# Fewer, larger DMAs around the RWKV systems of a hybrid decoder step

## The chip, the cores and the metric

The kernel runs on one core of one Trainium2 chip. The metric is the device time of one execution in microseconds. Each core has five engines that run their own instruction queues: PE (matrix products; its weight loads are shown as PEld), DVE (vector), ACT (scalar), POOL (GpSimd) and SP, which in this kernel issues every DMA.

## What is computed

One inference step of a two-layer trunk on 1104 tokens (64 sample tokens, 16 meta tokens, 1024 prompt tokens) of width 1024. Layer 0 is gated DeltaNet. Layer 1, which the change touches, is RWKV-7 time mixing over 16 heads of 64:

```python
rkvz = einsum('sbtd,sde->sbte', xs[:4], w_rkvz)      # r, k, v, z projections of mixed tokens
w = -softplus(-(w0 + tanh(xs[4] @ w1) @ w2)) - 0.5   # vector decay
a = sigmoid(a0 + (xs[5] @ a1) @ a2)
kk = l2norm((k * k_k).reshape(B, T, H, N))
k = k * (1.0 + (a - 1.0) * k_a)
decay = exp(-exp(w)); b = kk * a
def step(S, inp):                                     # per token, state S is [value, key]
    S = S*d_t + einsum('bhvk,bhk->bhv', S, -kk_t)[..., None]*b_t + v_t[..., None]*k_t
    return S, einsum('bhvk,bhk->bhv', S, r_t)
```

After it come a per-head GroupNorm, a bonus term, a SiLU gate, an output projection and a final RMSNorm.

## The kernel before

Tokens lie along the free dimension, features on the 128 partitions, in three segments of 384, 384 and 336 tokens. The recurrence is done in chunks of 64 tokens: within a chunk the rank-one updates form a unit lower triangular system, whose inverse is needed before the recurrence can run. A *system* here is one pair of heads (8 pairs, `p`) in one segment (3, `s`): 24 systems, numbered `n = 8 * s + p`, each with 6 chunks of 64 tokens for two heads.

Layer 1 has three stages.

1. `keys_decay_rate` projects the keys and computes the decay sums (cumulative, per chunk) and `a`, and writes them to DRAM: `kd`, `csd`, `ad`, each [8, 128, 1152]. Zeros are put in the last 48 columns of all but `csd`.
2. `layer1` runs 24 projections (`project`: r, then v, then z, 8 feature tiles each; `rd`, `vd`, `zd` in DRAM). After projections 1, 4, 7, 10 and 13 of them stands a call of `rwkv_inverse`, which does five systems (the last call four). For every system, or *item*, it loads `cs`, `a` and `k` (`rwkv_load`, an item ahead), scales the keys to `kk` (`skk` in the profile), takes exponentials of the decay sums on ACT (`sDp`, `siD`), squares the keys (`sgl`), forms alpha = kk * Dp (`sal`, DVE L1285, with column fixes on POOL) and bk = kk * a * iD in place (POOL L1310, DVE L1311), and stores both to DRAM (`ald`, `bkd`) for stage 3. PE makes the 12 products of 64x64 that give the triangular blocks (`fL`) and the squared norms of the keys per head (`frss`, a product with a mask of two columns, `hmask`). The blocks go to DRAM (`rltd`), the norms through a copy (`rkc`, DVE L1327) too (`rssd`). After five items, `block_scale` loads the norms and inverts them, `inverse_blocks` loads all 32x32 diagonal blocks of the batch in one tile (`invA`), `inverse32` inverts them on DVE with 62 small steps (`invtmp`, `invT`, L452 and L454), and the results go through DRAM (`r_t`, `r_u`) into `T1n` and into the tiles `sTT`, one per system, in four DMAs for each. `inverse_merge` then joins the blocks (`mY`, `invY`, `mU`), POOL scales them (L1336), and they are stored (`ttd`).
3. `wave` runs the recurrence, the output projection and the final norm. `rwkv_front` starts one system every two steps: it loads `cs`, `k`, `a`, `r`, `v` (`fld...`), `alpha` and `bk` (into `AR` and `BK`) and later the inverse (`rTT`).

All tiles come from pools. A tag with `bufs` buffers is reused round-robin: the next user of a buffer waits until its last reader is done, a DMA among them. The order of instructions on each engine is fixed at compile time: a scheduler simulates the program's timeline and takes what is ready by priority, roughly program order; in the wave, PE's order is written by hand. So moving a call in the program, or changing a size, gives a new order on every engine. The instructions that split weights in a high and a low part (`whi` on ACT L86, `wlo` on POOL L90) and mix tokens (`mixs`) run beside the inverse.

`inverse_blocks` and the tag `invA` at L465 serve the RWKV batches alone; layer 0 has a buffer of that name of its own (L641) and calls `inverse32` directly.

Of the kernel before, what the change touches and what calls it, by code (L numbers as in the profile page):

```python
# [35 lines left out]
class Builder:  # L36
# [76 lines left out]
    def consts(self):  # L113
        nc, i = self.nc, self.i
        cp = self.cp = self.ctx.enter_context(self.tc.tile_pool(name="consts", bufs=1))
        self.psum = ExitStack()
        self.psum_pool()
        t = self.t
        self.ident = t(cp, [128, 128], "ident")
        make_identity(nc, self.ident)  # L120
        vals = [1.0, -0.5]
        self.cvals = t(cp, [128, len(vals)], "cvals")
        self.cidx = {}
        for n, v in enumerate(vals):
# [5 lines left out]
        nc.gpsimd.memset(self.hmask, 0.0)  # L130
        for h in (0, 1):
            nc.gpsimd.memset(self.hmask[64 * h:64 * h + 64, h:h + 1], 1.0)
# [324 lines left out]
    def inverse_blocks(self, name, ltd, scale_blk, pool, TT, T1n, L21, nth):  # L457
# [7 lines left out]
        A = self.t(pool, [128, 1024], "invA", 2)[0:nb]  # L465
# [746 lines left out]
    def rwkv_masks(self, ap, first=False):  # L1212
# [14 lines left out]
        if first:  # L1227
            self.m_strs2 = t(ap, [128, 64], "m_strs2")
            mask(self.m_strs2, True)
            return  # L1230
# [17 lines left out]
    def rwkv_open(self):  # L1248
        self.rk2 = self.t(self.cp, [128, 144], "rk2")
        self.csd, self.ad, self.rd, self.vd, self.zd, self.kd = (self.dram([8, 128, 1152], n) for n in  # L1250
                                                                 ("csd", "ad", "rd", "vd", "zd", "kd"))
        self.ttd, self.ald, self.bkd = (self.dram([24, 128, 384], n) for n in ("ttd", "ald", "bkd"))

    def rwkv_load(self, n, pool, tag, names):
        nc, t = self.nc, self.t
        s, p = divmod(n, 8)
        c0 = SEGS[s][0]
        ld = {}
        for nm in names:
            d = {"cs": self.csd, "a": self.ad, "r": self.rd, "v": self.vd, "k": self.kd}[nm]  # L1260
            ld[nm] = t(pool, [128, 384], tag + "ld" + nm, 2 if nm in "rv" or tag == "s" else 1)
            nc.sync.dma_start(ld[nm], d[p][:, c0:c0 + 384])
        return ld

    def rwkv_keys(self, p, ld, pool, tag):

        nc, t = self.nc, self.t
        kk = t(pool, [128, 384], tag + "kk", 2)
        self.act(kk, ld["k"], AF.Identity, scale=self.pcol["rwkv_k_k"][:, p:p + 1])
        return kk, *self.rwkv_decays(ld, pool, tag)  # L1270

    def rwkv_decays(self, ld, pool, tag):
# [4 lines left out]
        self.act(Dp[:, 1:385], ld["cs"], AF.Exp, scale=-self.DEC)  # L1277
        self.act(iD, ld["cs"], AF.Exp, scale=self.DEC)
# [14 lines left out]
    def rwkv_inverse(self, b, pool):  # L1293
# [4 lines left out]
        ltd, ssd = self.dram([nth, 128, 64], f"rltd{b}"), self.dram([nth, 128], f"rssd{b}")  # L1298
        for q, n in enumerate(items):
            s, p = divmod(n, 8)  # L1300
            names = ("cs", "a", "k")
# [6 lines left out]
            al = t(pool, [128, 6, 64], "sal", 1)  # L1308
            self.alpha(al, kk, Dp, s, nc.vector)
            nc.gpsimd.tensor_tensor(kk, kk, ld["a"], op=ALU.mult)  # L1310
            nc.vector.tensor_tensor(kk, kk, iD, op=ALU.mult)  # L1311
            nc.sync.dma_start(self.ald[n], al.rearrange("p c k -> p (c k)"))
            nc.sync.dma_start(self.bkd[n], kk)
            gp = self.ps("f", 2, "L")
            ssp = self.ps("f", 2, "rss")
            for c in range(6):
                for h in (0, 1):
                    a = 64 * h
                    self.mm(gp[a:a + 64, 64 * c:64 * c + 64], kk[a:a + 64, 64 * c:64 * c + 64], al[a:a + 64, c, :])
            self.mm(ssp[0:2, 0:384], self.hmask, sq)  # L1320
# [5 lines left out]
            kc = t(pool, [2, 384], "rkc", 1)  # L1326
            nc.vector.tensor_copy(kc, ssp[0:2, 0:384])  # L1327
# [12 lines left out]
    def rwkv_front(self, p, s):  # L1340
# [11 lines left out]
        ld = self.rwkv_load(P.n, fp, "f", ("cs", "k", "a", "r", "v"))  # L1352
# [7 lines left out]
        nc.sync.dma_start(AR[:, 0].rearrange("p c k -> p (c k)"), self.ald[P.n])  # L1360
        nc.sync.dma_start(BK[:, :, 1, :], self.bkd[P.n].rearrange("p (c k) -> p c k", k=64))
# [439 lines left out]
    def layer1(self, ctx, right, stay, xa, xb, x):  # L1801
# [9 lines left out]
        for n, (m, k) in enumerate(todo):  # L1811
# [3 lines left out]
            if n in (1, 4, 7, 10, 13):  # L1815
                self.rwkv_inverse((1, 4, 7, 10, 13).index(n), ip)
# [160 lines left out]
```

## Time and profile before

| | |
|---|---|
| median of 3 runs | 2365.65 us (2362.40 to 2366.57) |
| the profiled execution | 2362.64 us, span 2360.9 us |
| busy: PE, PEld | 2167.1 us (92%), 1961.9 us (83%) |
| busy: DVE, ACT, POOL | 1571.2 us (67%), 1282.6 us (54%), 949.4 us (40%) |
| mean granted TensorE clock | 0.964 |
| DMA | 308.9 MB in 499,719 packets, 45.6% of 16 engines' span |

Times in the profile are microseconds from the span's start. A line of a group reads: source line, engine, operation, out<-in by the program's names, shape, count, then busy time and mean ns of one, then idle time of that engine just before and what ended it. A line of the chain of time begins with start and duration. A line of waits reads: engine and tile that waited, what it waited for, total us, times, the longest. A line "min/median/max" gives durations in ns. "issue" means that the profile shows nothing waited for. SPq lines are DMA issues; their duration is the time to issue, not to land.

### The profile page before, as it was taken

What the parts mean: (1) busy time and instruction counts of PE and PEld (TensorE: products, weight loads), DVE (VectorE), ACT (ScalarE), POOL (GpSimd) and SP (SyncE); (2) the same over time, 40 slices, a digit from 0 to 9 for tenths busy, and PEclk for the clock granted to TensorE, in tenths of its full rate; (3) what the DMA queues carried; (4) which work ended last, traced back from release to release, by engine and by line L of the source; (5) the groups of instructions that cost most, each with busy time, mean ns of one, the idle gap of its engine ahead of it and who ended that gap; (6) DMA issues with size and microseconds to landing.
All of it is one profiled execution on the core that took longest, in us unless ns stands there. A gap on an engine that the chain in (4) does not pass through costs nothing. (4 is left out here: it accounts for less than half of the span.)

```text
span 2360.9 us, 54503 instructions
## 1 busy us (share of the span) xinstructions
PE 2167.1 (92%) x19737; PEld 1961.9 (83%) x19737; DVE 1571.2 (67%) x4219; ACT 1282.6 (54%) x3599; POOL 949.4 (40%) x1318
## 2 busy tenths in 40 slices
PE   6989999999999999999999999999888888899886
PEld 5888989889898989898989998887777866778775
DVE  6878677685858686774345833479878456667754
ACT  5455545564656555456333746646444355677763
POOL 3445333443435353434232523446445423344433
PEclk9999999999999999999999999998999998999998
DMA  3423332323233333335152145577774654677753
GB/s 113 107 76 104 88 94 78 101 75 105 78 101 91 90 102 88 109 90 184 48 163 83 52 163 175 182 199 197 188 181 130 178 160 143 178 220 227 215 153 126
DMA packets 499719, 308.89 MB, mean 131 GB/s; under 512 B 208089, under 2 KB 484826, under 8 KB 499450
## 3 DMA queue, kind: packets, MB, share of 16 engines
q1 hardware_dynamic: 499450, 305.41, 45.6%
q8 instruction: 156, 2.56, 0.5%
q14 instruction: 113, 0.93, 0.1%
HBM read 209.97 MB, written 95.33 MB: 129 GB/s over the span
## 5 line engine op out<-in xcount | busy, mean ns | idle before, releaser
L90 POOL TENSOR_TENSOR wlo<-wraw,whi 128x512 fp32r<-128x512 f32 (+2 forms) x252 | 332.4, 1322 | 359.8 <-ACT whi L86 334.4
L76 PE MATMUL d<-xc,whi 128*128 128x384 f32 (+2 forms) x910 | 260.2, 344 | 8.1 <-ACT whi L86 3.6
L86 ACT CAST whi<-wraw 128x512 fp32r<-128x512 f32 (+2 forms) x252 | 151.7, 603 | 138.8 <-PE dq L76 50.7
L419 DVE SCALAR_TENSOR_TENSOR cvy<-raw,cw,cvy 128x408 f32<-128x408 f32 (+2 forms) x288 | 178.3, 632 | 15.7 <-ACT cvy L62 13.8
L452 DVE TENSOR_TENSOR invtmp<-invA,invT 72x31 f32<-72x31 f32 (+31 forms) x403 | 172.7, 429 | 18.7 <-POOL invT L447 8.0
L76 PEld LDWEIGHTS d<-xc,whi 128*128 128x128 f32 (+1 forms) x910 | 168.9, 193 | 15.2 <-ACT whi L86 4.7
L454 DVE TENSOR_TENSOR invT<-invT,invtmp 72x31 f32<-72x31 f32 (+31 forms) x403 | 172.3, 428 | 6.6
L76 PE MATMUL dz<-xc,whi 128*128 128x384 f32 (+1 forms) x480 | 149.4, 343 | 0.0
L76 PE MATMUL dv<-xc,whi 128*128 128x384 f32 (+1 forms) x480 | 146.8, 335 | 0.0
L76 PE MATMUL d<-xa,whi 128*128 128x384 f32 (+3 forms) x450 | 141.4, 348 | 4.1 <-DVE xa L90 2.8
L76 PE MATMUL d<-xc,wlo 128*128 128x384 f32 (+2 forms) x428 | 143.9, 345 | 0.7 <-POOL wlo L90 0.7
L868 POOL TENSOR_SCALAR Sb<-Sb,eglb 128x128 f32<-128x128 f32 x128 | 80.4, 645 | 87.6 <-DMA Sb<-in_state_gdn 36.6
L76 PE MATMUL dz<-xa,whi 128*128 128x384 f32 (+1 forms) x288 | 100.3, 348 | 0.0
L76 PE MATMUL dv<-xa,whi 128*128 128x384 f32 (+1 forms) x288 | 99.9, 347 | 0.1
L76 PEld LDWEIGHTS d<-xa,whi 128*128 128x128 f32 (+1 forms) x450 | 85.2, 194 | 12.8 <-issue 5.2
L76 PEld LDWEIGHTS dz<-xc,whi 128*128 128x128 f32 x480 | 89.5, 192 | 0.8
L76 PEld LDWEIGHTS dv<-xc,whi 128*128 128x128 f32 x480 | 88.6, 188 | 0.5 <-issue 0.4
L76 PE MATMUL d<-xa,wlo 128*128 128x384 f32 (+3 forms) x252 | 86.6, 344 | 0.0
L62 ACT ACTIVATE o<-rA,gcol 128x128 f32<-128x128 f32 x128 | 46.6, 372 | 72.6 <-DVE S L779 72.0
L76 PE MATMUL d<-xh,wlo 128*128 128x384 f32 (+1 forms) x256 | 83.9, 343 | 2.0 <-POOL wlo L90 2.0
L76 PEld LDWEIGHTS d<-xc,wlo 128*128 128x128 f32 (+1 forms) x428 | 82.1, 194 | 4.0 <-issue 1.9
L76 PE MATMUL d<-xh,whi 128*128 128x384 f32 (+1 forms) x256 | 84.5, 344 | 0.5 <-ACT whi L86 0.5
(509 smaller groups left out, 7012.3 us busy)
## 6 DMA issues: line engine op xcount, KB each, us to landing
wraw<-in_gdn_w_in SPq DMA_DIRECT2D x96, 256.0 KB
wraw<-in_rwkv_w_rkvz SPq DMA_DIRECT2D x80, 256.0 KB
Sb<-in_state_gdn SPq DMA_DIRECT2D x64, 256.0 KB
wraw<-in_rwkv_w_o SPq DMA_DIRECT2D x40, 256.0 KB
E<-drow SPq DMA_DIRECT2D x24, 384.0 KB
attn<-drow SPq DMA_DIRECT2D x24, 384.0 KB
wraw<-in_gdn_w_out SPq DMA_DIRECT2D x36, 256.0 KB
out_s_gdn<-Sb SPq DMA_DIRECT2D x32, 256.0 KB
```

Of the source, the lines that this page charges most:

```text
L62: return self.nc.scalar.activation(out, in_, func, bias=bias, scale=scale, **kw)
L76: self.nc.tensor.matmul(out, lhsT, rhs, start=start, stop=stop)
L86: nc.scalar.copy(hi, x)
L90: e.tensor_tensor(lo, x, hi.bitcast(F32), op=ALU.subtract)
L419: nc.vector.scalar_tensor_tensor(y[:, 0:wd], raw[:, k:k + wd], cw[k], y[:, 0:wd], op0=ALU.mult, op1=ALU.add)
L452: nc.vector.tensor_tensor(tmp, A[:, j, j + 1:32].unsqueeze(2).broadcast_to([nb, n, m]), Tv[:, j, 0:m].unsqueeze(1).broadcast_to([nb, n, m] ...
L454: nc.vector.tensor_tensor(Tv[:, j + 1:32, 0:m], Tv[:, j + 1:32, 0:m], tmp, op=ALU.subtract)
L868: nc.gpsimd.tensor_scalar(Sb[:, u], Sb[:, u], self.eglb[:, hv, 4 * g + u:4 * g + u + 1], None, op0=ALU.mult)
```

## The change

Decay sums, a and keys share one DRAM tensor with three planes per pair and are loaded by one DMA; so do r and v. Alpha and bk share one tile and one store. The norms of the keys are taken with a mask of 32 columns in three products of 128 tokens each, put on partitions 0, 32 and 64 of one PSUM tile; a copy of 96x128 gathers them for five systems, and six DMAs store them once a batch. The five tiles `sTT` become one, loaded by four DMAs a batch. `invA` and `kk` get one buffer in place of two. The mask is made with the other masks of the stage. `rwkv_inverse` is called after projections 0, 3, 6, 9 and 12.

```diff
-        self.hmask = t(cp, [128, 2], "hmask")           # in consts(), with its three memsets
+            self.hmask = t(ap, [128, 32], "hmask")      # in rwkv_masks(first=True), with its three memsets
@@ inverse_blocks
-        A = self.t(pool, [128, 1024], "invA", 2)[0:nb]
+        A = self.t(pool, [128, 1024], "invA", 1)[0:nb]
@@ rwkv_open
-        self.csd, self.ad, self.rd, self.vd, self.zd, self.kd = (self.dram([8, 128, 1152], n) for n in
-                                                                 ("csd", "ad", "rd", "vd", "zd", "kd"))
-        self.ttd, self.ald, self.bkd = (self.dram([24, 128, 384], n) for n in ("ttd", "ald", "bkd"))
+        self.cakd, self.rvd, self.zd = (self.dram([8, 128, n, 1152], m) for n, m in ((3, "cakd"), (2, "rvd"), (1, "zd")))
+        self.csd, self.ad, self.kd = (self.cakd[:, :, x] for x in range(3))
+        self.rd, self.vd = (self.rvd[:, :, x] for x in range(2))
+        self.zd = self.zd[:, :, 0]
+        self.ttd, self.abd = self.dram([24, 128, 384], "ttd"), self.dram([24, 128, 768], "abd")
@@ rwkv_load
-        for nm in names:
-            d = {"cs": self.csd, "a": self.ad, "r": self.rd, "v": self.vd, "k": self.kd}[nm]
-            ld[nm] = t(pool, [128, 384], tag + "ld" + nm, 2 if nm in "rv" or tag == "s" else 1)
-            nc.sync.dma_start(ld[nm], d[p][:, c0:c0 + 384])
+        for g in names:
+            d = {"cak": self.cakd, "rv": self.rvd}[g]
+            x = t(pool, [128, len(g), 384], tag + "ld" + g, 1 if g == "cak" and tag == "f" else 2)
+            nc.sync.dma_start(x, d[p][:, :, c0:c0 + 384])
+            for j, nm in enumerate(g):
+                ld[nm] = x[:, j]
@@ rwkv_keys
-        kk = t(pool, [128, 384], tag + "kk", 2)
+        kk = t(pool, [128, 384], tag + "kk", 1)
@@ rwkv_inverse
+        kc = t(pool, [96, 5, 128], "rkc", 1)
...
-            al = t(pool, [128, 6, 64], "sal", 1)
+            ab = t(pool, [128, 2, 384], "sal", 1)
+            al, bk = ab[:, 0].rearrange("p (c k) -> p c k", k=64), ab[:, 1]
             self.alpha(al, kk, Dp, s, nc.vector)
             nc.gpsimd.tensor_tensor(kk, kk, ld["a"], op=ALU.mult)
-            nc.vector.tensor_tensor(kk, kk, iD, op=ALU.mult)
-            nc.sync.dma_start(self.ald[n], al.rearrange("p c k -> p (c k)"))
-            nc.sync.dma_start(self.bkd[n], kk)
+            nc.vector.tensor_tensor(bk, kk, iD, op=ALU.mult)
+            nc.sync.dma_start(self.abd[n], ab.rearrange("p x k -> p (x k)"))
...
-            self.mm(ssp[0:2, 0:384], self.hmask, sq)
+            for g in range(3):
+                self.mm(ssp[32 * g:32 * g + 32, 0:128], self.hmask, sq[:, 128 * g:128 * g + 128])
...
-            kc = t(pool, [2, 384], "rkc", 1)
-            nc.vector.tensor_copy(kc, ssp[0:2, 0:384])
-            nc.sync.dma_start(ssd[6 * q:6 * q + 6].rearrange("c (h i) -> h c i", h=2), kc.rearrange("h (c i) -> h c i", c=6))
+            nc.vector.tensor_copy(kc[:, q], ssp[0:96, 0:128])
+        sv = ssd.rearrange("(q g c) (h i) -> g h q c i", g=3, c=2, h=2)
+        for g in range(3):
+            for h in (0, 1):
+                nc.sync.dma_start(sv[g, h:h + 1], kc[32 * g + h:32 * g + h + 1, 0:len(items)].rearrange("h q (c i) -> h q c i", c=2))
...
-        TT = [t(pool, [128, 6, 64], "sTT", 3) for _ in items]
+        TA = t(pool, [128, 30, 64], "sTT", 1)
+        TT = [TA[:, 6 * q:6 * q + 6] for q in range(len(items))]
...
-        self.inverse_blocks(f"r{b}", ltd, blk, pool, TT, T1n[:, 0:nth], L21[:, 0:nth], nth)
+        self.inverse_blocks(f"r{b}", ltd, blk, pool, [TA[:, 0:nth]], T1n[:, 0:nth], L21[:, 0:nth], nth)
@@ rwkv_front
-        ld = self.rwkv_load(P.n, fp, "f", ("cs", "k", "a", "r", "v"))
+        ld = self.rwkv_load(P.n, fp, "f", ("cak", "rv"))
...
-        nc.sync.dma_start(AR[:, 0].rearrange("p c k -> p (c k)"), self.ald[P.n])
-        nc.sync.dma_start(BK[:, :, 1, :], self.bkd[P.n].rearrange("p (c k) -> p c k", k=64))
+        nc.sync.dma_start(AR[:, 0].rearrange("p c k -> p (c k)"), self.abd[P.n][:, 0:384])
+        nc.sync.dma_start(BK[:, :, 1, :], self.abd[P.n][:, 384:768].rearrange("p (c k) -> p c k", k=64))
@@ layer1
-            if n in (1, 4, 7, 10, 13):
-                self.rwkv_inverse((1, 4, 7, 10, 13).index(n), ip)
+            if n in (0, 3, 6, 9, 12):
+                self.rwkv_inverse((0, 3, 6, 9, 12).index(n), ip)
```

More of the change, by code (lines that the diff above doesn't have):

```diff
@@ L128, in consts @@
         nc.gpsimd.memset(self.ones, 1.0)
-        self.hmask = t(cp, [128, 2], "hmask")
-        nc.gpsimd.memset(self.hmask, 0.0)
-        for h in (0, 1):
-            nc.gpsimd.memset(self.hmask[64 * h:64 * h + 64, h:h + 1], 1.0)
         self.bmask = t(cp, [128, 8], "bmask")
@@ L1229, in rwkv_masks @@
             mask(self.m_strs2, True)
+            self.hmask = t(ap, [128, 32], "hmask")
+            nc.gpsimd.memset(self.hmask, 0.0)
+            for h in (0, 1):
+                nc.gpsimd.memset(self.hmask[64 * h:64 * h + 64, h:h + 1], 1.0)
             return
@@ L1276, in rwkv_decays @@
         nc.gpsimd.memset(Dp[:, 0:1], 1.0)
-        self.act(Dp[:, 1:385], ld["cs"], AF.Exp, scale=-self.DEC)
-        self.act(iD, ld["cs"], AF.Exp, scale=self.DEC)
+        self.act(Dp[:, 1:385], ld["c"], AF.Exp, scale=-self.DEC)
+        self.act(iD, ld["c"], AF.Exp, scale=self.DEC)
         return Dp, iD
@@ L1298, in rwkv_inverse @@
         ltd, ssd = self.dram([nth, 128, 64], f"rltd{b}"), self.dram([nth, 128], f"rssd{b}")
+        kc = t(pool, [96, 5, 128], "rkc", 1)
         for q, n in enumerate(items):
             s, p = divmod(n, 8)
-            names = ("cs", "a", "k")
+            names = ("cak",)
             ld = self.ahead or self.rwkv_load(n, pool, "s", names)
```

3 lines of the change are left out of this document (2 added, 1 removed).

## The prediction

> **What bounds the kernel now.** I read the page's busy times first, then the six stretches in which the code's stages lie, then what PE waited for in the stretch that the change touches.
>
> ```profile
> PE 2167.1 (92%) x19737; PEld 1961.9 (83%) x19737; DVE 1571.2 (67%) x4219; ACT 1282.6 (54%) x3599; POOL 949.4 (40%) x1318
> ...
> 1470.00:1490.00 20.00, 16.04 (x70) 15.10 (x70) 15.14 (x24) 18.39 (x41) 13.62 (x26) 0.74 0.55 177
> 1490.00:1590.00 100.00, 98.67 (x739) 88.22 (x737) 56.41 (x115) 49.41 (x106) 41.77 (x65) 1.00 0.73 201
> 1590.00:1820.00 230.00, 202.73 (x2122) 176.09 (x2122) 199.38 (x419) 114.42 (x250) 117.92 (x150) 0.92 0.67 173
> 1820.00:1865.00 45.00, 41.69 (x389) 39.37 (x388) 15.59 (x29) 16.65 (x34) 19.26 (x38) 0.92 0.62 178
> 1865.00:2361.00 496.00, 421.60 (x5952) 353.26 (x5952) 302.92 (x1011) 296.71 (x850) 190.12 (x210) 0.94 0.60 177
> ```
>
> The columns after the length are the busy times of PE, PEld, DVE, ACT and POOL, then the granted TensorE clock. PE is the bound: 92% of the span. The RWKV systems are built between 1470 and 1865, beside the r, v and z projections. There PE is busy 16.0 + 98.7 + 202.7 + 41.7 = 359 of 395 us, so it stands idle for 36 us. It also loses clock: (1 - 0.74) x 20 + (1 - 0.92) x 275 = 27 us, an upper estimate, since idle time is in it. Nothing that removes waiting here can win more than about 63 us. From 1590 to 1820 DVE is nearly as full as PE (199 of 230 us). After 1865 runs the recurrence ("the wave"), of which the change touches the loads alone.
>
> ```profile
> PE fL L76 <- DVE skk L1311: 9.8, 5, 4.1
> PE mU L76 <- issue: 4.7, 3, 2.9
> PE mY L76 <- DMA T1n<-r_t: 4.1, 2, 3.8
> PE d L76 <- ACT whi L86: 3.6, 2, 2.8
> PE mY L76 <- issue: 2.9, 1, 2.9
> PE frss L76 <- DVE invtmp L452: 2.4, 1, 2.4
> ...
> 1476.21 0.52 PE L76 MATMUL d<-xh,whi 128*128 128x384 f32 x1
> 1476.53 0.52 PE L76 MATMUL d<-xh,wlo 128*128 128x384 f32 x1
> ...
> 1494.12 0.34 PE L76 MATMUL d<-xh,whi 128*128 128x384 f32 x1
> 1494.29 0.33 PE L76 MATMUL d<-xh,wlo 128*128 128x384 f32 x1
> ```
>
> The waits of PE in 1470 to 1865 are few, each a matmul of the inverse that stands at the head of PE's fixed order while its input is late. Such a stall costs twice: matmuls of one shape start 0.32 us apart just after the stall at 1473 and 0.17 us apart at 1494. So the price of one stall is its 2 to 4 us and a few more.
>
> **The change, part by part.** The profiled execution took 2362.64 us (span 2360.9 and 1.7 around it). It is near the low end of the three runs, 3.0 us under their median 2365.65. I sum against 2362.64 and add the 3.0 at the end.
>
> *Norms in three column tiles.* Per item, one fp32 product of a 128x2 mask with 384 columns becomes three of a 128x32 mask with 128 columns, written to partitions 0, 32 and 64.
>
> ```profile
> 1609.22 0.92 PE L76 MATMUL fL<-sal,skk 64*64 64x64 f32 x24
> 1610.07 0.81 PE L76 MATMUL frss<-sgl,hmask 128*2 128x384 f32 x2
> 1610.81 0.62 PE L76 MATMUL d<-xa,whi 128*128 128x384 f32 x2
> ...
> L76 PEld LDWEIGHTS frss<-sgl,hmask x48: 80/82/84, 1499.6 to 1754.5; 128*2 128x2 f32 x48
> L1327 DVE COPY rkc<-frss 2x384 f32<-2x384 f32 x24 | 13.1, 544 | 1.0 <-PE frss L76 0.2
> L437 DVE COPY lasts<-flast 27x128 f32<-27x128 f32 x32 | 8.7, 271 | 0.3
> ```
>
> The product holds PE from 1610.07 to 1610.81, 0.74 us, and 24 items make 17.8 us. The same columns pass in all. If the three tiles ran one after the other, nothing is won and four more weight loads of 82 ns are added: at worst 24 x 4 x 0.082 = 7.9 us lost. If all three run side by side, two thirds go: 11.8 us won. The nearest row is fL above: 24 records of 64 columns start within 0.85 us, 35 ns each, while frss passes 2 x 384 columns in 0.74 us, about 1.04 columns per ns, at which 64 would take 62 ns. So products in different tiles of the array overlap 1.75-fold here, though those differ in rows too. I take 17.8 x (1 - 1/1.75) = 7.6 us won, on PE, the bound. The Trainium skill (TensorE: Matmul & The Clock Gate, Measured speedup vs the span model) gives 2.38 for three column tiles of 32, by which the term would be an estimated 10.3 us. Against the change speaks its page TensorEngine Tiling (Array Packing), Key Properties: a change of tiling mode drains the array; no row here shows the price of a drain alone, and the trace already goes from 64-wide tiles to whole ones at 1610.
>
> The copy of the norms gets short: 128 columns on 96 partitions in place of 384 on 2. The row of 27x128 out of PSUM says 271 ns for 544, so DVE wins 24 x 0.273 = 6.6 us. Most of it lies beside PE's work. By the 14% of DVE's idle time from 1590 to 1820 it is a second bound only at times; I take 1 us, between 0 and 6.6.
>
> *Fewer issues on SP.* Loads of decay sums, a and keys: 72 become 24. Stores of alpha and bk: 48 become 24. Loads of the inverted blocks: 96 become 5 x 4 = 20. Front loads in the wave: 120 become 48. Stores of norms: 24 become 30. That is 214 fewer. Bytes and pieces stay as they are.
>
> ```profile
> L1262 SPq DMA_DIRECT2D sldcs<-csd x24: 319/400/1271, 1470.7 to 1716.9; - x24
> L480 SPq DMA_DIRECT2D T1n<-r_t x10: 326/524/3883, 1585.7 to 1824.2; - x10
> L486 SPq DMA_DIRECT2D sTT<-r_u x96: 302/439/1656, 1592.0 to 1841.2; - x96
> ```
>
> At a median of 0.40 us this is 214 x 0.40 = 86 us of SP's time. A 120 KB load in the same small pieces (T1n) costs 0.52 us to issue, the 24 KB one (sTT) 0.44, so a merged one is cheap. But little of it is waited for. Of PE's rows above, those that a late load ends or may end are mY (4.1 and 2.9) and mU (4.7), 11.7 us. I take a quarter, 3 us, between 0 and 11.7.
>
> *One tile for five systems.* Before, three buffers served five systems, and the fourth waited for the first to be stored.
>
> ```profile
> L484 POOL MEMSET sTT<- 32x192 f32 x48 | 12.1, 252 | 26.6 <-DMA ttd<-sTT 25.0
> L446 POOL MEMSET invT<- 120x1024 f32 x4 | 3.8, 953 | 9.1 <-DMA r_t<-invT 7.9 <-ACT xa L86 1.3
> ...
> 1826.76 5.64 SPq L486 DMA_DIRECT2D sTT<-r_u  x12
> 1835.53 0.47 PE L76 MATMUL mU<-sTT,invY 32*32 32x32 f32 x18
> ```
>
> POOL stood 25 us behind those stores. That goes, and 48 memsets of 0.25 us become 10 of about 0.9 (the invT row, nearly the same width): 12 us become 9. POOL has room (118 of 230 us), and none of PE's rows above ends on it, so I count 1 us, between 0 and 3. What comes instead: the first merge needs all of a batch, 480 KB, where it had 288 KB loaded in the 8.8 us from 1826.76 to 1835.53. This is the first rival; in the sum it is 0, since the merges that come after no longer wait for stores.
>
> *Alpha and bk in one buffer.* The store now begins when bk is done, and the next alpha needs the buffer back.
>
> ```profile
> 1480.48 1.27 DVE L1311 TENSOR_TENSOR skk<-skk,siD 128x384 f32<-128x384 f32 x1
> ...
> 1511.51 0.56 DVE L1311 TENSOR_TENSOR skk<-skk,siD 128x384 f32<-128x384 f32 x1 [1.77 <-POOL skk L1310]
> 1512.19 0.45 SPq L1313 DMA_DIRECT2D bkd<-skk  x1
> 1516.61 0.58 DVE L1285 TENSOR_TENSOR sal<-skk,sDp 128x384 f32<-128x384 f32 x1 [4.54 <-PE fL L76]
> 1517.29 0.62 ACT L62 ACTIVATE skk<-sldk,pcol 128x384 f32<-128x384 f32 x1 [0.22 <-DMA bkd<-skk]
> ...
> 1751.25 1.61 DVE L1311 TENSOR_TENSOR skk<-skk,siD 128x384 f32<-128x384 f32 x1
> ```
>
> A 192 KB store issued at 1512.19 released its buffer at 1517.29, 5.1 us later. With twice the bytes (1.0 us more at the 201 GB/s of this stretch) it lands 6.1 us after its issue and 6.8 after bk began. Alpha of the next item began 5.1 us after bk. So DVE would stand 1.7 us longer. Of the 23 such distances (the first of the 24 bk at 1480.48, the last at 1751.25), 15 are under 6.8 us, short by 1.4 us on average: 21 us of DVE, with its copies, mixes and inversion steps queued behind. In the first half DVE has 44 us of room in 100 and PE is full without it; I take a quarter, 5 us lost, between 0 and 21. The single buffer of keys costs nothing: kk is no longer stored, and its next writer waits for bk alone, which ended at 1512.07, 4.5 us ahead of the next alpha. The single invA buffer neither: only the RWKV batches use that line, and they are some 60 us apart (T1n's issues, 1585.7 to 1824.2, over four gaps).
>
> *Calls one projection earlier.* The batches follow projections 0, 3, 6, 9 and 12.
>
> ```profile
> L76 PE MATMUL mU<-sTT,invY x576: 184/191/258, 1601.6 to 1850.4; 32*32 32x32 f32 x192
> ```
>
>  Work on PE is the same; the last batch, whose last product begins at 1850, within 15 us of the stage's end, gets some 12 us more projections behind it (72 matmuls at 0.17). The compiler draws up each engine's order anew from its own estimate of times, so each stall may go or come. I take two of PE's stalls gone, at about 3 us each (the longest of the six rows above are 2.4 to 4.1): 6 us won; bounds are 18 us either way, three stalls with their slow clock.
>
> *The wave.* A front's cs, a and k come in one load, when the last reader of all three is done.
>
> ```profile
> 2061.85 1.10 DVE L1366 TENSOR_TENSOR k<-k,fldk 128x384 f32<-128x384 f32 x1
> 2063.29 0.62 SPq L1262 DMA_DIRECT2D fldk<-kd  x1
> 2075.53 0.53 ACT L62 ACTIVATE fDp<-fldcs 128x384 f32<-128x384 f32 x1
> ```
>
> That reader ends at 2062.95 and the next front begins at 2075.53: 12.6 us for a load whose third took about 5 in the busiest stretch. Hidden. SP's shorter queue may bring weights sooner; 1 us won, between 4 lost and 6 won.
>
> **Sum.** Won: 7.6 + 1 + 3 + 1 + 6 + 1 = 19.6. Lost: 5. Net 14.6, so 2348.0 for the profiled execution and 2351 for the median, 0.6% less.
>
> **The rivals.** Differences under 0.2%, 4.7 us, can't be told from none, the runs before lying 4.2 us apart.
>
> *The merged load of inverted blocks becomes PE's wait.* All 480 KB must land ahead of a batch's first mU. By the row of 8.8 us for 288 KB that is 14.7 us, 5.9 later. If PE's order keeps mU where it was, five batches cost 29.5 us, less the 14.6: 2365.65 + 14.9 = 2380.6, and the slow clock adds to it. For it: PE stood 3.8 us before mY for a 120 KB load of the same pieces. Against: the planner spaces mU behind its loads, and the later merges come sooner. It decides once PE stands over 3 us ahead of the first mU in most batches. 0.26, with a worse plan of other kinds counted here.
>
> *The alpha wait reaches PE in full.* 21 us lost in place of 5: 1.4 lost in all, 2367, no difference. For it: fL behind skk is already PE's largest row. Against: PE was full where the distances are shortest. 0.14.
>
> *The replanned stage loses most of its stalls.* Half of the 63 us go: 2365.65 - 32 - 7.6 = 2326. The plan would have to be better everywhere; 0.08.
>
> *The tiles don't run side by side.* Then the first term is between 0 and 7.9 lost: 2359 to 2366. That is a bound in the range more than a case; it is counted with the forecast and with no difference.
>
> **How the numbers follow.** The forecast, 2351, has 0.52 with its own range 2336 to 2360 (below: five stalls gone rather than two, 9 us, the tiles at their best, 4, and two late loads more, 2; above: no stall and no late load gone, 6 + 3). With the fourth case, 0.60 is faster, 0.14 no difference, 0.26 slower. The range reaches to the first and third rivals: 2327 to 2381, since under 2 in 10 lie beyond.
>
> **What would show it.** Right: frss holds PE for some 0.4 us per item, rkc is near 0.27 us, sTT memsets no longer wait for ttd, PE's idle time from 1470 to the stage's end is under 36 us, the wave as long as before (496 us). Wrong: three frss products one after the other; PE idle ahead of mU in each batch; alpha waiting for the store of alpha and bk with fL late behind it; or a wave longer by over 5 us, which none of my terms allows.

## The result, and the profile after

The changed kernel takes 2374.17 us (14 runs), the kernel before 2365.75 (14 runs), both medians. The ratio over all these runs is 1.0049, 95% interval 1.0032 to 1.0067: 0.5% slower, some 12 us, where 0.6% faster was forecast. (The medians alone differ by 8.4 us.)

The profiled execution of after has a span of 2378.7 us, 17.8 more than before. More than half of that seems to say nothing of the change. The store of zeros into z, at the start of layer 1, comes 9.9 us later, though of the work ahead of it only the making of the mask was changed; over the profiles of all 20 kernels here that store begins between 1351.7 and 1363.5. So everything below is measured from it. Four groups of before and after, from the timeline by tile (ns, then the first and the last start):

```profile
L1172 SPq DMA_DIRECT2D zd<-zpad x1: 645/645/645, 1353.6 to 1353.6; - x1
L1163 SPq DMA_DIRECT2D zd<-ev x16: 319/338/573, 1783.3 to 1863.7; - x16
L1337 SPq DMA_DIRECT2D ttd<-sTT x24: 319/341/573, 1605.6 to 1853.1; - x24
```

```profile
L1168 SPq DMA_DIRECT2D zd<-zpad x1: 918/918/918, 1363.5 to 1363.5; - x1
L1159 SPq DMA_DIRECT2D zd<-ev x16: 319/339/2238, 1794.9 to 1874.4; - x16
L76 PE MATMUL mU<-sTT,invY x576: 184/191/258, 1601.7 to 1880.5; 32*32 32x32 f32 x192
L1346 SPq DMA_DIRECT2D ttd<-sTT x24: 319/382/1803, 1611.0 to 1882.4; - x24
```

The last projection ends 510.1 us after the zeros before and 510.9 after. But the last merge (`mU`), which began 13.3 us ahead of that, begins 6.1 us behind it. Three stretches each, cut at the last store of z and at the first and last `fG` (a product of the wave, made 24 times for each system), before and then after (columns: length, then busy time of PE, PEld, DVE, ACT and POOL, clock, DMA share, GB/s):

```profile
1470.00:1863.70 393.70, 357.98 (x3311) 317.90 (x3311) 286.52 (x584) 197.57 (x426) 191.42 (x274) 0.93 0.67 180
1863.70:1871.50 7.80, 3.18 (x16) 2.54 (x14) 3.66 (x5) 3.00 (x7) 4.54 (x6) 0.78 0.54 156
1871.50:2266.10 394.60, 350.73 (x5238) 293.82 (x5239) 257.29 (x860) 253.12 (x718) 152.90 (x167) 0.96 0.64 189
```

```profile
1479.90:1874.40 394.50, 348.47 (x3251) 317.41 (x3249) 280.78 (x572) 192.98 (x414) 181.89 (x215) 0.93 0.63 173
1874.40:1893.40 19.00, 12.73 (x172) 11.45 (x172) 8.46 (x15) 5.91 (x16) 9.66 (x27) 0.68 0.78 231
1893.40:2287.30 393.90, 349.89 (x5238) 294.91 (x5239) 257.63 (x864) 254.40 (x721) 153.26 (x170) 0.97 0.63 188
```

The projections take as long as before although the last merges have left them, PE's idle time in them grew from 35.7 to 46.0 us, and the gap ahead of the wave grew from 7.8 to 19.0. The wave is no longer. What the prediction said to look at, in the timeline and by tile:

```profile
1511.70 0.91 PE L76 MATMUL fL<-sal 64*64 64x64 f32 x24
1512.54 0.42 PE L76 MATMUL frss<-sgl,hmask 128*32 128x128 f32 x6
1512.89 0.42 PE L76 MATMUL d<-xc,wlo 128*128 128x336 f32 x1
```

```profile
L1332 DVE COPY rkc<-frss x24: 276/281/289, 1503.5 to 1779.6; 96x128 f32<-96x128 f32 x24
L1336 SPq DMA_DIRECT2D rssd<-rkc x30: 576/700/847, 1539.6 to 1783.7; - x30
```

The norms hold PE for 0.35 us per item in place of 0.74, so the three tiles do run side by side; a change of tile shape ahead of them and one behind are in these 0.35 us. The copy is at 281 ns. And the waits of DVE, then of ACT, from 1470 to 1885 (us, times, longest):

```profile
DVE sal L1289 <- DMA abd<-sal: 19.0, 9, 5.2
DVE sal L1317 <- POOL skk L1316: 18.0, 10, 4.3
...
DVE bblk L498 <- DMA bblk<-rssd: 13.1, 4, 7.0
DVE invA L466 <- DMA invA<-rltd: 11.6, 4, 5.8
```

```profile
ACT skk L62 <- DVE sal L1317: 40.8, 21, 3.9
ACT sDp L62 <- DVE sal L1289: 33.8, 13, 4.5
ACT sDp L62 <- DMA sldcak<-cakd: 7.8, 2, 5.3
```

Each of the change's edits has a wait of its own here. Which of them the time hangs on, the waits don't say.

### The profile page after: what moved, and what is told of

It reads as the page before. It is cut to its first block, busy times and chain, and to the rows that moved or that the text cites. A ratio compares the mean times of both kernels' runs of the same rounds, so it can differ in the third digit from the quotient of the medians.

```text
span 2378.7 us, 54233 instructions
## 1 busy us (share of the span) xinstructions
PE 2170.6 (91%) x19833; PEld 1973.6 (83%) x19833; DVE 1568.8 (66%) x4219; ACT 1280.8 (54%) x3599; POOL 945.9 (40%) x1280
```

## The experiments

Three theories were tested. *Theory 1*: with one `invA`, a batch is loaded only when the batch before has been stored, so the inversions stand in a row, the last merges fall behind the last projection, and the wave starts late (its buffers take the place of the inverse's). *Theory 2*, the prediction's second rival: alpha waits for the shared store. *Theory 3*, formed when theory 1 no longer explained the loss: an item's merged load lands late.

In the table, "us" is the ratio less one, times 2361 us (the kernel before beside them: medians of 2359.8 to 2362.1). Stage is the time from the zeros to the wave's first `fG`, gap the part of it after the last store of z, wave the time from the first to the last `fG`, all of the one profiled execution, which lies up to 9 us from its kernel's median (2380.8 for 2371.5 with the items' loads merged, 2361.6 for 2369.2 with the calls earlier).

Of the kernels made from the one before, only that with one `invA` has its edit alone. All others also have the joined DRAM tensors and a mask made in the later place, and where their fronts' loads are apart, these stand in another order (decay sums, a, keys in place of decay sums, keys, a). What this does alone was not measured, so it is part of each of these effects; the row with the norms has it too and comes to -2.

| kernel | ratio, 95% interval | us | stage | gap | wave |
|---|---|---|---|---|---|
| before | 1 | 0 | 517.9 | 7.8 | 394.6 |
| after | 1.0049, 1.0032 to 1.0067 | +12 | 529.9 | 19.0 | 393.9 |
| before, one `invA` | 1.0073, 1.0049 to 1.0098 | +17 | 533.7 | 30.5 | 392.7 |
| before, merged loads | 1.0070, 1.0045 to 1.0095 | +17 | 525.4 | 12.5 | 402.6 |
| before, items' loads merged | 1.0060, 1.0036 to 1.0084 | +14 | 520.7 | 11.8 | 402.3 |
| before, fronts' loads merged | 1.0033, 1.0012 to 1.0053 | +8 | 516.5 | 1.2 | 400.5 |
| before, shared store, one `kk` | 1.0048, 1.0030 to 1.0066 | +11 | 523.2 | 8.9 | 392.5 |
| before, calls earlier | 1.0038, 1.0020 to 1.0056 | +9 | 520.1 | 0.7 | 393.5 |
| before, norms | 0.9990, 0.9974 to 1.0005 | -2 | 518.3 | 7.4 | 394.8 |
| before, norms, calls earlier | 1.0051, 1.0032 to 1.0069 | +12 | 525.7 | 4.9 | 397.1 |
| before, tiles, a store per item | 0.9981, 0.9964 to 0.9999 | -4 | 510.3 | 5.2 | 398.1 |
| the same, copies on ACT | 1.0016, 0.9997 to 1.0036 | +4 | 515.6 | 21.0 | 396.7 |
| after, old `invA`, `sTT` | 1.0076, 1.0056 to 1.0095 | +18 | 529.7 | 18.9 | 399.8 |
| the same, a store per item | 1.0011, 0.9994 to 1.0029 | +3 | 510.4 | 8.6 | 402.9 |
| after, old calls | 1.0064, 1.0044 to 1.0084 | +15 | 534.1 | 26.6 | 393.4 |
| after, all loads apart | 0.9985, 0.9966 to 1.0004 | -4 | 514.6 | 17.8 | 392.9 |
| after, items' loads apart | 0.9978, 0.9958 to 0.9998 | -5 | 514.5 | 20.1 | 389.7 |
| all loads apart, old `invA`, `sTT`, store per item | 0.9984, 0.9968 to 1.0000 | -4 | 502.3 | 7.2 | 398.9 |
| the same, alpha and bk apart, two `kk` | 0.9976, 0.9964 to 0.9989 | -6 | 508.0 | 5.9 | 393.2 |
| last but one, fronts' loads merged | 0.9955, 0.9942 to 0.9967 | -11 | 501.0 | 5.4 | 395.8 |

**One invA alone.** On the kernel before:

```diff
-        A = self.t(pool, [128, 1024], "invA", 2)[0:nb]
+        A = self.t(pool, [128, 1024], "invA", 1)[0:nb]
```

> The kernel before with one edit: invA gets one buffer. Theory 1 (the inversions became serial: a batch's invA may be loaded only when the batch before has stored its own, so every inversion on DVE starts some 14 to 18 us after the one before ended, the last batch's merges fall behind the last projection, and the wave, whose buffers need the inverse's pool closed, starts late): 2373 to 2379 us, most of the change's loss by itself; first load of the wave some 15 to 25 us later. As compiled, PE's order has no projection product left behind the last mU (59 in the kernel before). Rival (alpha waits for the shared store): invA is innocent, 2366 +-3. The prediction's own term (single invA costs nothing): 2366 +-3.

17 us slower, by a line that the prediction had put at nothing. The last batch's turn in the timelines of before, of after, and the gap of this run:

```profile
1760.44 1.06 SPq L469 DMA_DIRECT2D invA<-rltd  x2
1766.18 2.09 ACT L472 COPY invA<-invT 120x1024 f32<-120x1024 f32 x1
1767.88 1.20 DVE L470 TENSOR_TENSOR invA<-invA,bblk 96x1024 f32<-96x1024 f32 x1
```

```profile
1810.82 2.09 ACT L468 COPY invA<-invT 120x1024 f32<-120x1024 f32 x1 [6.57 <-DVE invT L450]
1812.93 0.34 SPq L471 DMA_DIRECT2D r_u<-invA  x1
1819.33 1.47 SPq L465 DMA_DIRECT2D invA<-rltd  x2
1824.43 1.22 DVE L466 TENSOR_TENSOR invA<-invA,bblk 96x1024 f32<-96x1024 f32 x1 [1.77 <-DMA invA<-rltd]
```

```profile
1858.70:1889.20 30.50, 15.01 (x222) 13.31 (x222) 9.32 (x17) 6.91 (x17) 10.18 (x29) 0.56 0.62 167
```

Before, the next batch's blocks are loaded 5.7 us ahead of the copy that ends a batch, and DVE goes on 1.7 us after that copy began. With one buffer the chain copy, store, load, scale takes 13.6 us (in this run 17.2), in which no inversion runs. The wave's first product comes 30.5 us after the last projection, half of it idle, at a mean clock of 0.56. For this edit alone, theory 1 holds.

**invA and sTT put back in the changed kernel.**

```diff
-        A = self.t(pool, [128, 1024], "invA", 1)[0:nb]
+        A = self.t(pool, [128, 1024], "invA", 2)[0:nb]
...
-        TA = t(pool, [128, 30, 64], "sTT", 1)
-        TT = [TA[:, 6 * q:6 * q + 6] for q in range(len(items))]
+        TT = [t(pool, [128, 6, 64], "sTT", 3) for _ in items]
...
```

> The changed kernel with invA back at two buffers; for the room that takes, sTT is back at three tiles for five systems. If theory 1 is the whole of it, this is 2358 to 2366. If the items themselves come later in the changed kernel (single kk, alpha and bk in one buffer, merged load), the last mU stay behind the last projection, as PE's compiled order has it here too, and it is 2369 to 2377 although the gaps between the inversions are closed. Theory 2 (alpha's wait): no change from the changed kernel, 2374.

Nothing came back: 2379.5 us, above all that was expected. The gap stayed (18.9), so the buffer isn't the whole of it: the items themselves come late. The last `fL` begins 400.6 us after the zeros before, 410.8 in after (1774.3) and 434.9 here.

**Merged loads alone, and norms alone.** The hunk of `rwkv_load` with its DRAM tensors, on the kernel before; and the hunks of the mask, of the three products and of `rkc`, on the kernel before. Of each a cut:

```diff
...
-            nc.sync.dma_start(ld[nm], d[p][:, c0:c0 + 384])
+            nc.sync.dma_start(x, d[p][:, :, c0:c0 + 384])
...
```

> The kernel before with the merged loads alone: decay sums, a and keys in one DMA, r and v in one. The prediction's term for SP's issues gives 1 to 3 us won: 2363 to 2365. By PE's compiled order nothing is left behind the last mU (59 in the kernel before), so if the transition to the wave is what counts, it is slower: 2368 to 2376, with the systems' items later in the stage.

```diff
...
-            self.mm(ssp[0:2, 0:384], self.hmask, sq)
+            for g in range(3):
+                self.mm(ssp[32 * g:32 * g + 32, 0:128], self.hmask, sq[:, 128 * g:128 * g + 128])
...
```

> The kernel before with the norms alone: three column tiles, copy of 96x128, six stores a batch. The prediction's terms give 7.6 on PE and about 1 on DVE: 2357. If the tiles win PE time but the six late stores hold block_scale (31 projection products left behind the last mU, for 59), the transition gives 3 to 5 us back: 2361 to 2364. Nothing won at all: 2366.

The loads lose 17 us where 1 to 3 were to be won. The norms win PE's time and lose most of it again. PE's waits from 1470 to 1872 in that run, and its first two stretches:

```profile
PE fL L76 <- DVE skk L1315: 13.0, 6, 4.2
PE fbpp L73 <- DMA invR<-rssd: 4.9, 2, 3.3
```

```profile
1477.30:1871.80 394.50, 350.24 (x3415) 321.37 (x3413) 282.50 (x582) 198.30 (x425) 179.74 (x276) 0.93 0.65 178
1871.80:1879.20 7.40, 2.23 (x10) 1.64 (x8) 3.54 (x5) 1.99 (x5) 3.54 (x5) 0.73 0.60 154
```

PE is busy for 7.7 us less in the projections, which are 0.8 us longer: idle time went from 35.7 to 44.3. The transpose of the norms (`fbpp`) waits 4.9 us for their load, against 0.9 before; six stores are now issued in a row at the batch's end.

**Shared store alone; calls alone; norms with calls; one store per item.** Each on the kernel before, as said under the table. The first, with the hunk of `kk`, cut:

```diff
...
-            al = t(pool, [128, 6, 64], "sal", 1)
+            ab = t(pool, [128, 2, 384], "sal", 1)
...
```

> The kernel before with alpha and bk in one buffer and one store, and kk in one buffer, alone. Rival 2 (alpha waits for the shared store): DVE waits some 15 to 21 us for it, and all of it would reach PE: 2366 plus 10 to 20, 2376 to 2386. The prediction's term: 5 lost, 2367 to 2371. Theory 1 (only what lets the last merges fall behind the last projection costs much; here 13 projection products are left behind the last mU, for 59 before): 2366 to 2370.

The second, and as the third the second together with the norms:

```diff
-            if n in (1, 4, 7, 10, 13):
+            if n in (0, 3, 6, 9, 12):
...
```

> The kernel before with the calls of the batches one projection earlier alone. PE's compiled order leaves 110 projection products behind the last mU, for 59 before. The prediction's term: 6 us won, 2356 to 2360. Theory 1: the inverse's pool closes some 9 us earlier against the last projection, the wave's first loads land before it ends, and the 7.8 us from the last projection to the wave's first product go down to 2 to 4: 2358 to 2362. If the stage's stalls only move: 2362 +-3.

> The kernel before with the norms in column tiles (six stores a batch) and the calls one projection earlier; invA and kk keep two buffers, alpha and bk, and all loads, stay apart. 144 projection products are left behind the last mU. Theory 1 with the 9 us that the tiles save on PE: 2350 to 2356, less than both kernels. If PE's saved time turns into idle time, as it did with the norms alone: 2358 to 2362.

The fourth, the tiles with another copy and store:

```diff
-            nc.vector.tensor_copy(kc[:, q], ssp[0:96, 0:128])
+            kc = t(pool, [2, 384], "rkc", 1)
+            for g in range(3):
+                nc.vector.tensor_copy(kc[:, 128 * g:128 * g + 128], ssp[32 * g:32 * g + 2, 0:128])
+            nc.sync.dma_start(ssd[6 * q:6 * q + 6].rearrange("c (h i) -> h c i", h=2), kc.rearrange("h (c i) -> h c i", c=6))
```

> The kernel before with the norms in column tiles alone, but with three small copies to two partitions and one store per item as before, in place of six stores at the batch's end. If it was the six late stores that ate the 8 us of PE (PE waited 4.9 us for the norms' load in the run with the norms alone, for 0.9 before), this is 2354 to 2358. If the projection stage is set by another chain than PE's work, it is 2359 to 2362 like the norms alone. DVE has 24 x 3 copies more.

The shared store loses 11 us, but in its trace DVE waited for that store for 3.1 us in all, so this isn't theory 2. The earlier calls bring the merges 25 us ahead of the last projection and still lose 9; with the norms they lose 12. So early merges alone buy nothing. Both times every case of the expectation was missed: 2369.2 us where none went above 2365, and 2371.7 where theory 1 had at most 2356 and the other case 2362. The fourth is the first that is faster than before, by 4 us; its interval ends just short of no difference.

**Three tests of theory 1.** The changed kernel with `invA` and `sTT` put back and one store per item as above; the kernel before with tiles and a store per item, but

```diff
-                nc.vector.tensor_copy(kc[:, 128 * g:128 * g + 128], ssp[32 * g:32 * g + 2, 0:128])
+                nc.scalar.copy(kc[:, 128 * g:128 * g + 128], ssp[32 * g:32 * g + 2, 0:128])
```

and the changed kernel with its calls after 1, 4, 7, 10 and 13.

> The changed kernel with invA at two buffers, sTT at three tiles and one store of norms per item (three small copies); merged loads, the shared store of alpha and bk, the single kk, the column tiles and the earlier calls stay. 32 projection products are left behind the last mU, for 0 in the changed kernel and in the earlier run with invA and sTT put back. Theory 1 (it is the place of the last merges that costs): 2358 to 2364, though it holds three edits that lost 16, 11 and 9 us alone. If those losses add up, whatever the place of the last mU: 2380 or more. If only six late stores made the difference: 2370.

> The same as the run with column tiles and one store per item (2358.5), but the three small copies of each item go on ACT in place of DVE. As work this is nothing: ACT has some 140 of 274 us free in this stretch. But the compiled order leaves no projection product behind the last mU, for 39 in that run. Theory 1: 2368 to 2376, 10 to 17 us lost by the order alone. Rival (the edits cost by the waits that they add): 2356 to 2361.

> The changed kernel with the calls after projections 1, 4, 7, 10 and 13 as before. No projection product is left behind the last mU. Theory 1: no better, 2372 to 2380. If the calls' loss of 9 us, seen when they were moved alone, is a part of its own: 2363 to 2367.

The first came out at the upper end of what theory 1 had: three edits that lost 37 us alone are in it, and it is 3 us from before. The second moves 72 copies of 0.28 us to an engine with room; the merges fall behind the last projection, the gap goes from 5.2 to 21.0, and 8 us are lost (-4 to +4), less than the 10 to 17 of theory 1 and more than its rival had. The third is no better, as expected.

**The loads taken apart in the changed kernel.** (`k` is then the third of a front's loads, not the second.)

```diff
-            x = t(pool, [128, len(g), 384], tag + "ld" + g, 1 if g == "cak" and tag == "f" else 2)
-            nc.sync.dma_start(x, d[p][:, :, c0:c0 + 384])
             for j, nm in enumerate(g):
-                ld[nm] = x[:, j]
+                ld[nm] = t(pool, [128, 384], tag + "ld" + nm, 1 if g == "cak" and tag == "f" else 2)
+                nc.sync.dma_start(ld[nm], d[p][:, j, c0:c0 + 384])
```

> The changed kernel with decay sums, a, keys, r and v loaded one by one again. No projection product is left behind the last mU. Theory 1: no better, 2372 to 2378. If the loss of 16 us seen when the loads were merged alone is a part of its own: 2356 to 2360.

This broke theory 1 as the cause of the loss: the gap is still 17.8 us, and yet 16 us are won. The next three split it: the items' loads alone and the fronts' alone, merged in the kernel before; the items' alone apart in the changed one. The diff is that of the second and the third; the first has `"f"` in its first line. The fourth takes all loads apart and puts `invA`, `sTT` and the store per item back, as above.

```diff
+            if tag == "s":
+                for j, nm in enumerate(g):
+                    ld[nm] = t(pool, [128, 384], tag + "ld" + nm, 1 if g == "cak" and tag == "f" else 2)
+                    nc.sync.dma_start(ld[nm], d[p][:, j, c0:c0 + 384])
+                continue
```

> The kernel before with decay sums, a and keys of the systems' items in one load; the wave's front loads stay apart. Theory 3 (the merged load of an item lands late, and ACT's first step of the item waits for all 576 KB: 13.9 us in the run with both merged, 1.4 before): 2366 to 2372, the key stage's start to the wave's first product some 7 us longer than before, the wave as before. If the front's loads carry the loss: 2360 to 2363.

> The kernel before with the front loads of the wave merged (decay sums, a and keys in one, r and v in one); the stage before the wave has the compiled order of the kernel before. Theory 3: 2360 to 2363, no difference. If merged front loads make the wave 8 us longer, as it was in the run with both: 2367 to 2371.

> The changed kernel with the loads of the systems' items apart; the front loads stay merged. Theory 3: all 16 us that were won with both taken apart are won here: 2355 to 2361. If the gain came from the front loads: 2370 to 2376. As before, no projection product is left behind the last mU.

> The changed kernel with all loads apart, invA at two buffers, sTT at three tiles, and one store of norms per item; kept are the column tiles, the shared store of alpha and bk with a single kk, and the earlier calls. 34 projection products are left behind the last mU. Theories 1 and 3 (late last merges and late merged loads are the two losses): 2348 to 2356, below both kernels. If the shared store and the calls cost what they cost alone (11 and 9 us): 2366 or more.

The items' loads carry it: 14 us lost in the kernel before, 17 won back in the changed kernel (+12 to -5). The time of the first of these runs came as theory 3 had it, but not the place: the stage is 2.8 us longer, where 7 were expected, and the wave 7.7, where none was. Nor did theory 3 foresee that the fronts' loads alone cost 8 us, the wave 5.9 longer. How the items' loads may come to cost this, in the timeline of after and in its SP waits:

```profile
1532.13 1.02 POOL L1316 TENSOR_TENSOR skk<-skk,sldcak 128x384 f32<-128x384 f32 x1
1533.18 0.53 SPq L1264 DMA_DIRECT2D sldcak<-cakd  x1
...
1551.17 0.58 SPq L1264 DMA_DIRECT2D sldcak<-cakd  x1
1557.06 0.53 ACT L62 ACTIVATE sDp<-sldcak 128x384 f32<-128x384 f32 x1 [5.33 <-DMA sldcak<-cakd]
```

```profile
SPq L1264 <- POOL skk L1316: 24.1, 13, 6.0
```

in ACT's waits with the items' loads merged in the kernel before (1.4 and 0.5 us without):

```profile
ACT skk L62 <- DMA sldcak<-cakd: 15.0, 4, 6.2
ACT sDp L62 <- DMA sldcak<-cakd: 2.6, 2, 2.1
```

and in the changed kernel with the items' loads apart:

```profile
1495.98 0.62 ACT L62 ACTIVATE skk<-sldk,pcol 128x384 f32<-128x384 f32 x1 [0.35 <-DVE sal L1322]
1496.87 0.54 SPq L1266 DMA_DIRECT2D sldk<-cakd  x1
1497.51 0.45 SPq L1266 DMA_DIRECT2D sldc<-cakd  x1
...
1501.02 1.01 POOL L1321 TENSOR_TENSOR skk<-skk,slda 128x384 f32<-128x384 f32 x1
1502.76 0.38 SPq L1266 DMA_DIRECT2D slda<-cakd  x1
```

Apart, the keys' buffer is loaded again as soon as ACT has scaled the keys; decay sums follow 0.6 us later, and only `a` must wait for POOL's product; it goes out 5.9 us after the keys. SP stands in front of that product as often (24.4 us with all loads apart), but only `a` is behind it. Merged, all three are. In after, 16 of the 22 loads that have such a product ahead of them are issued within 0.1 us of its end, as the one at 1533 is, and the first step that reads a load begins 4.8 to 12.4 us after its issue. Apart, keys and decay sums are issued 3 to 12 us ahead of that product, and from the third item on their first reader comes some 10 us or more after the issue. So the merged load takes the lead that keys and decay sums had; these, which an item needs first, come with `a`, which it needs last. The load at 1551 is another case: its buffer was free at 1541 (the product at 1539.96 takes 1.01 us), but SP first issued the stores and loads of the batch's end, as it does with the loads apart. ACT then waited for all 576 KB and began 5.9 us after the issue.

These waits are smaller than the loss: ACT stands 9.5 us for the items' loads in after and 2.2 with them apart, 17.6 with them merged in the kernel before and 1.9 without. That the whole loss comes by this path isn't shown; each of these edits also gives a new order. A second wait goes with the merged loads. DVE waits 14.7 to 28.2 us for the shared store in the four kernels that have both, and 3.1 to 8.1 us in the five that have it with the items' loads apart. In the changed kernel with the items' loads apart, DVE's waits ahead of alpha are:

```profile
DVE sal L1294 <- PE fL L76: 9.6, 3, 4.4
...
DVE sal L1294 <- DMA abd<-sal: 4.0, 1, 4.0
```

The first was 1.7 us in after, the second 19.0. Whether part of the loss goes through that store is open; a kernel with 26.1 us of that wait, the changed one with old `invA`, `sTT` and a store per item, is only 3 us from before.

The 24 alphas show the row of items, in after, and in the kernel with the items' loads apart:

```profile
L1289 DVE TENSOR_TENSOR sal<-skk,sDp x24: 494/557/1371, 1488.7 to 1765.5; 128x384 f32<-128x384 f32 x24
```

```profile
L1294 DVE TENSOR_TENSOR sal<-skk,sDp x24: 494/552/1625, 1475.9 to 1733.8; 128x384 f32<-128x384 f32 x24
```

```profile
1470.50:1848.50 378.00, 336.48 (x3251) 307.62 (x3251) 275.96 (x568) 191.73 (x411) 179.29 (x211) 0.95 0.64 179
1848.50:1868.60 20.10, 11.82 (x173) 10.41 (x166) 8.80 (x15) 5.98 (x16) 10.11 (x27) 0.67 0.77 229
```

From the first alpha to the last 276.8 us become 257.9, and the two stretches up to the wave, in the last fence, are 398.1 us for 413.5 in after. As many products keep PE busy for 348.3 us up to the wave where after takes 361.2; the clock is at 0.95 for 0.93 in the projections.

**Two last runs, from the best kernel so far.** Alpha and bk apart with two `kk`; and, on the same kernel, only the fronts' loads merged again, by the diff of the items' loads above. A cut of the first:

```diff
-        kk = t(pool, [128, 384], tag + "kk", 1)
+        kk = t(pool, [128, 384], tag + "kk", 2)
...
-            nc.sync.dma_start(self.abd[n], ab.rearrange("p x k -> p (x k)"))
+            nc.sync.dma_start(self.ald[n], al.rearrange("p c k -> p (c k)"))
+            nc.sync.dma_start(self.bkd[n], bk)
...
```

> The best kernel of the last call (2355.9) with alpha and bk stored apart again and kk at two buffers: so the kernel before with the column tiles, one store of norms per item, and the earlier calls alone. If the shared store costs in every surrounding what it cost alone (11 us): 2343 to 2347. If its loss alone came from a worse plan, which the best kernel doesn't have: 2353 to 2362.

> The best kernel of the last call (2355.9) with the front loads merged again (decay sums, a and keys in one, r and v in one). If merged front loads cost as they did alone (8 us, the wave 6 us longer): 2361 to 2366. If they cost nothing, as in the changed kernel with the stage's loads apart (2354.9): 2353 to 2358.

Neither edit shows the loss that it had alone: 11 us for the shared store is 2 here, within the intervals, and the fronts' loads win 7 where they had lost 8, more than either case of the expectation. The last kernel takes 2349.0 us beside 2361.6 before, ratio 0.9955: it beats both. It keeps the column tiles, the shared store, the single `kk`, the earlier calls and the fronts' loads. Its stretches:

```profile
1472.10:1851.30 379.20, 343.87 (x3408) 313.31 (x3407) 284.22 (x627) 196.07 (x423) 180.09 (x270) 0.96 0.67 184
1851.30:1856.70 5.40, 2.14 (x13) 1.68 (x12) 2.62 (x5) 2.58 (x6) 1.57 (x5) 1.00 0.93 239
1856.70:2252.50 395.80, 352.10 (x5238) 297.46 (x5239) 259.20 (x864) 254.88 (x721) 155.90 (x171) 0.96 0.64 190
```

## Why the prediction was wrong, by its steps

- **Norms in column tiles: the mechanism right, its worth overrated.** 24 x (0.74 - 0.35) = 9.4 us of PE, for 7.6 forecast: 2.1-fold, nearer to the 2.38 of the Trainium skill (TensorE: Matmul & The Clock Gate, Measured speedup vs the span model) than to my 1.75. But it was credited in full as time on the bound. Alone it was worth 2 us, which can't be told from none, with one store per item 4; in the run with the norms alone, PE's 7.7 us of less work came with 8.6 us more of idle time.
- **Fewer issues on SP: the step that failed.** I priced a merged load by its issue (0.52 us), called it cheap and put down 3 us won. In the wave I did ask when "the last reader of all three is done"; for the items I didn't. Merging the items' loads cost 14, 17 and 13 us in three surroundings (kernel before; changed kernel; changed kernel with `invA`, `sTT` and stores per item put back). The traces show why it can cost, the lost lead and the wait for the whole; by which wait all of it comes is open. The Trainium skill (DMA: Bandwidth & Descriptors, Anatomy of one DMA) has a fixed cost of some 2 us per DMA, which speaks for merging; for 576 KB its fit, measured on another engine's path, gives an estimated 3.4 us, where 5.9 passed here.
- **invA with one buffer "costs nothing": wrong.** Alone it costs 17 us. I compared the batches' spacing (some 60 us) with nothing; what counts is that the next load was issued ahead of the end of the inversion (1760.4 against 1766.2). In the changed kernel, undone together with `sTT` and the six stores, it was worth 9 us (+12 to +3); with the items' loads apart 5 (-5 to -11), inside the intervals; with all loads apart nothing (-4 and -4). Its share of these wasn't measured.
- **Alpha's wait: size right by luck, place open.** DVE waited 19.0 us in nine items, for 21 in fifteen. But the sum was worked out for this edit on the kernel before, and there the wait is 3.1 us; waits of 14.7 us and more came only with the items' loads merged too, which the sum didn't have. Alone the edit lost 11 us all the same, by a path that isn't known; in the best kernel its loss can't be told from none. `kk`: ACT waits 40.8 us for bk, and no run shows what that alone costs.
- **One sTT tile.** POOL's memsets wait for stores once, 6.1 us, where it was 25.0 us in eleven times, and the first rival did not come: PE waited 1.2 us for the merged load of inverted blocks. Its worth alone wasn't tried.
- **Calls earlier: 6 won, 9 lost.** In the changed kernel they seem to win 3 (ratio 1.0064 without them, 1.0049 with), inside the intervals. A forecast of stalls gone through a new order had no ground in the trace.
- **The wave: right for this kernel** (393.9 for 394.6), not for the kernel before: there the merged fronts' loads, which I called hidden, cost 8 us alone, the wave 5.9 longer. They cost nothing in the changed kernel with the items' loads apart (-4 and -5) and win 7 in the best one. (The "about 5" us in that sum were those of a 192 KB store, not of a load.) Across the runs the wave lies between 389.7 and 402.9. In those above 398 us PE is busy 2 to 7 us longer with the same products, and the clock of the first 130 us doesn't tell them apart: 0.88 in waves of 392.9 and of 402.9 us. Why is open; with the items' loads merged in the kernel before, most of the loss in the profile lies there (402.3), though in an execution 9 us above the median, and I can't say by what path.

The account that the runs allow, in one order of undoing: the best kernel's 11 us won, less 5 for `invA`, `sTT` and the six stores, less 17 for the items' loads, is 12 lost but for rounding. The parts done alone on the kernel before (+17, +17, +11, +9, -2) add up to 52, so they don't add. That each upsets one balanced order, which can be upset only once, would fit, and so does the 8 us that moving 72 small copies to ACT cost; it wasn't tested further.

## What to carry to other kernels

Here a merged load waited for the last reader of all that it replaced and was there only as a whole: merge what is freed and needed at the same time, and keep apart what the next step needs first. Before a buffer is halved, look whether the next load is issued ahead of the last use of the one before; the row of loads beside the row of uses shows it. Where an order is fixed at compile time and nearly full, an edit's effect alone says little of its effect among others, so try parts by taking them out of the whole as well as by putting them in.

## What was not expected of the hardware

A store of a gathered row from one partition took 700 ns to issue, the old store from two partitions 264; so six stores a batch cost SP more (30 x 0.70 = 21 us) than one per item (24 x 0.26 = 6 us):

```profile
L1328 SPq DMA_DIRECT2D rssd<-rkc x24: 241/264/583, 1501.3 to 1758.3; - x24
```

And with the same work ahead of it but for the mask, layer 1 began at times spread over 12 us of the span (1351.7 to 1363.5), which is as much as the whole effect: a single profile could not have told it.
